# The weights of a block of keys in an mLSTM begun two units ahead of the products that read them

## The chip, the cores and the metric

The kernel runs on one core of a Trainium2 chip. It computes a whole encoder block for one sequence of 512 positions and a model width of 2048. The metric is the time of one execution on the device in microseconds (us), the median of several runs.

## The reference, cut to what matters

The block takes the root mean square norm of the input, projects it with one wide matrix, gives the columns to two branches (a Hyena branch of long convolutions and an mLSTM branch of 4 heads), merges the branches and ends with a gated feed-forward network. All is fp32. The change stands in the mLSTM branch, which runs forward and backward over the sequence:

```python
def mlstm_direction(q, k, v, i_pre, f_pre):
...
    dlog = b[..., :, None] - b[..., None, :] + ig[..., None, :]
    dlog = jnp.where(lower, dlog, -jnp.inf)
...
    s = jnp.einsum('bhcjd,bhcsd->bhcjs', qc, kc) * jnp.exp(dlog - m_j[..., None])
    inter_w = jnp.exp(inter - m_j)
    num = (jnp.einsum('bhcjs,bhcsv->bhcjv', s, vc)
           + inter_w[..., None] * jnp.einsum('bhcjk,bhcvk->bhcjv', qc, C_prev))
    den = jnp.sum(s, axis=-1) + inter_w * jnp.einsum('bhcjk,bhck->bhcj', qc, n_prev)
    h = num / jnp.maximum(jnp.abs(den), jnp.exp(-m_j))[..., None]
```

The reference works in chunks of 128 with a carried state. The kernel does a head in the closed form that this unrolls to: each query sees every key up to it (or from it on, backward), with the weight q·k/16 times the exponential of a difference of gate sums. With 512 positions there are 4 blocks of 128 keys, and the denominator is had from a column of ones that stands beside v.

## The kernel before, in words

**Products.** An fp32 product is done as three matmuls of split operands (`mm3`, lines 85 to 88): every operand is held as a rounded high part and the rest as a low part. ScalarE casts the high part, VectorE subtracts to get the low one, TensorE multiplies high by high, high by low, low by high. All these matmuls carry line 83 in the profile. The tiles tell them apart: `mm` are the sums of the projection in PSUM, `sd` those of the side work.

**Two streams.** The main stream is the projection, `w_in_cols`: group by group of 256 weight columns, one unit of the stream being 12 matmuls of 128x512 (2 blocks of 128 columns, 2 of 128 rows, 3 matmuls each). Its weights come by DMA and are split (lines 182 and 183) two units ahead of their use, into 4 buffers each for `wh` and `wl`. The side stream is the Hyena and mLSTM work on what the projection has delivered. `drive` (line 291) runs one projection unit, then lets the side stream go on until what it yields adds up to 2.6 per unit: the numbers that `mlstm` yields are the price of the piece just written, and so the order in which the two streams' instructions are written down. A scheduler then sets each engine's order: by when, in its own plan of the execution, the operands of an instruction are there, and, where several are, by the order of writing.

**A head.** `mlstm(h)` (line 893) does a head: it splits q and k (line 948 splits v), makes S, 4 blocks of q·k products, then works through 8 units, 4 blocks of keys forward and 4 backward. Unit n has two parts:
- `weights` (line 953) makes the weights of the block of keys: the exponential (line 957, ScalarE, over 512 to 128 columns), a select that puts zeros over the triangle of the block's own 128 columns (line 960, GpSimd), the product with S (line 962, VectorE), the cast to the high part `pH` (line 965, ScalarE) and the subtraction for the low part `pL` (line 966, VectorE). This is a chain of five over three engines; its tiles are `g`, from a pool of 24.
- The products (line 987): for the block of queries of the unit, over the blocks of keys so far, `mm3` of 128x258 into one `sd` tile. That is 1, 2, 3, 4 block products forward and the same backward, 20 in a head, 60 matmuls. After them the sum is divided: line 990 (ScalarE, into `dn`), 991 and 992 (VectorE), then line 995 (ScalarE, forward) or 997 (VectorE, backward, added to the forward result). Line 1003 transposes the result of the head.

In the loop (line 972) unit n writes the chain of unit n + 1 first and then its own products. So the chain of a unit is written one unit ahead of its products, and the chain of unit 0 before the loop. Each unit yields 1.5, the part before the loop 1.

**Where the heads lie.** In the profile the four heads' units run at 389.8 to 416 us (head 0, between two convolutions), 662.7 to 699 (head 1), 723 to 751 (head 2) and 766 to 786 (head 3). During head 1 another side stream, `combos_x` (line 1070), works as well: it prepares operands for the merge of the branches with VectorE's lines 1065 to 1084. Its operations and the mLSTM's take turns.

Of the kernel before, what the change touches and what calls it, by code (L numbers as in the profile page):

```python
# [34 lines left out]
def hybrid_block_kernel(ctx, tc, x, norm1_w, w_in, conv_w, conv_b, filt_w1, filt_b1, filt_freq1,  # L35
# [43 lines left out]
    def sd_ps():  # L79
        return new(psd, "sd")  # L80
# [4 lines left out]
    def mm3(o, aH, aL, bH, bL, start, stop):  # L85
        mm(o, aH, bH, start, False)
        mm(o, aH, bL, False, False)
        mm(o, aL, bH, False, stop)
# [273 lines left out]
    def gt(dt=F32, shape=(P, L)):  # L362
        t = vt(dt)[:, 0:2, 0:258].rearrange("p b c -> p (b c)")[:, 0:L]
        return t if len(shape) == 2 else t.rearrange("p (b c) -> p b c", b=shape[1])

    def vt(dt=F32R):
        n_tile[0] += 1
        return pr.tile([P, 2, 258], dt, tag="g", name=f"g_{n_tile[0]}", bufs=NG)
# [9 lines left out]
    def gsplit(src, shape=(P, L)):  # L378
        h = gt(F32R, shape)
        l = gt(F32R, shape)  # L380
        nc.scalar.copy(h, src)
        nc.vector.tensor_tensor(l, src, h.bitcast(F32), ALU.subtract)
        return h, l
# [498 lines left out]
    def fetch_qk(h):  # L882
        raw = []
        for src in (d_q, d_k):
            for j in range(2):
                t = gt()
                nc.gpsimd.dma_start(t, src[2 * h + j])
                raw.append(t)
        return raw
# [3 lines left out]
    def mlstm(h, following=None):  # L893
        yield from need("gates")
        if h in fetched_qk:
            raw = fetched_qk.pop(h)
        else:
            yield from need(("qk", h))
            raw = fetch_qk(h)
            yield "pause"  # L900
        qs, ks = [], []
        for dst in (qs, ks):
            for j in range(2):
                dst.append(gsplit(raw.pop(0)))
                yield .7

        def load_row(d):
            t = gt()
            nc.gpsimd.dma_start(t, d_rows[4 * d + h:4 * d + h + 1].to_broadcast([P, L]))
            return t  # L910

        def load_v():
            raw = []
            for b in range(2):
                t = gt()
                nc.gpsimd.dma_start(t.rearrange("p (b c) -> p b c", b=2),
                                    d_v[h][2 * b:2 * b + 2].rearrange("b p c -> p b c"))
                raw.append(t)
            return raw

        early = ("v", h) in done
        if early:
            raw = load_v()
            row = load_row(0)
        yield "pause"
        S = []
        for sb in range(4):
            ps = sd_ps()
            ss = slice(sb * P, (sb + 1) * P)
            for j in range(2):  # L930
                mm3(ps, ks[j][0][:, ss], ks[j][1][:, ss], qs[j][0], qs[j][1], j == 0, j == 1)
            t = gt()
            nc.scalar.activation(t, ps, AF.Copy, scale=1.0 / 16)
            S.append(t)
            yield .3
        if not early:
            yield from need(("v", h))
            raw = load_v()
            row = load_row(0)
            yield "pause"  # L940
        V = []
        for t in raw:
            vh, vl = vt(), vt()
            nc.gpsimd.memset(vh[:, :, 256:258].bitcast(F32), 1.0)
            nc.gpsimd.memset(vl[:, :, 256:258].bitcast(F32), 0.0)
            src = t.rearrange("p (b c) -> p b c", b=2)
            nc.scalar.copy(vh[:, :, 0:256], src)
            nc.vector.tensor_tensor(vl[:, :, 0:256], src, vh[:, :, 0:256].bitcast(F32), ALU.subtract)
            for k in range(2):
                V.append((vh[:, k, :], vl[:, k, :]))  # L950
            yield .7

        def weights(d, sb, row):

            js = slice(sb * P, L) if d == 0 else slice(0, (sb + 1) * P)
            e = gt()
            nc.scalar.activation(e[:, js], row[:, js], AF.Exp, bias=a_col[:, d, sb, h:h + 1], scale=-1.0)
            own = e[:, sb * P:(sb + 1) * P]
            sign = 1 if d == 0 else -1
            nc.gpsimd.affine_select(own, own, pattern=[[sign, P]], compare_op=ALU.is_ge, fill=0.0,  # L960
                                    base=0, channel_multiplier=-sign)
            nc.vector.tensor_tensor(e[:, js], e[:, js], S[sb][:, js], ALU.mult)  # L962
            pH = gt(F32R)
            pL = gt(F32R)
            nc.scalar.copy(pH[:, js], e[:, js])
            nc.vector.tensor_tensor(pL[:, js], e[:, js], pH[:, js].bitcast(F32), ALU.subtract)
            return pH, pL


        units = [(0, sb) for sb in (0, 1, 2, 3)] + [(1, sb) for sb in (3, 2, 1, 0)]  # L970
        acc_t = [gt(), gt()]
        nxt = weights(*units[0], row)
        row_b = load_row(1)
        yield 1
        W = {}
        for n, (d, jb) in enumerate(units):
            if n == 4:
                W = {}
            if n == 5 and ("qk", following) in done:
                fetched_qk[following] = fetch_qk(following)  # L980
            W[jb] = nxt
            if n < 7:
                nxt = weights(*units[n + 1], row if n < 3 else row_b)
            num = sd_ps()
            js = slice(jb * P, (jb + 1) * P)
            for i, (sb, (pH, pL)) in enumerate(W.items()):
                mm3(num[:, 0:258], pH[:, js], pL[:, js], *V[sb], i == 0, i == len(W) - 1)
            n_tile[0] += 1
            dn = pr.tile([P, 1], F32, tag="dn", name=f"dn_{n_tile[0]}", bufs=3)
            nc.scalar.activation(dn, num[:, 256:257], AF.Abs)  # L990
            nc.vector.tensor_scalar(dn, dn, em_col[:, d, jb, h:h + 1], None, ALU.max)
            nc.vector.reciprocal(dn, dn)
            to = acc_t[jb // 2][:, (jb % 2) * 256:(jb % 2) * 256 + 256]
            if d == 0:
                nc.scalar.activation(to, num[:, 0:256], AF.Copy, scale=dn)
            else:
                nc.vector.scalar_tensor_tensor(to, num[:, 0:256], dn, to, ALU.mult, ALU.add)
            yield 1.5
        for vb in range(2):
            ps = sd_ps()  # L1000
            for tb in range(4):
                c0 = (tb % 2) * 256 + vb * P
                nc.tensor.transpose(ps[:, tb * P:(tb + 1) * P], acc_t[tb // 2][:, c0:c0 + P], ident)  # L1003
            t = gt()
            nc.scalar.copy(t, ps)
            nc.gpsimd.dma_start(d_yb[2 * h + vb], t)
        yield .3
# [4 lines left out]
    def need(key):  # L1012
        while key not in done:
            yield "wait"

    def stream_a():
        yield from gate_rows()
        yield from need("filter")
        for kind, n in (("hy", 0), ("hy", 1), ("hd", 0), ("hy", 2), ("hy", 3)):
            yield from hyena(n) if kind == "hy" else mlstm(n)  # L1020
        ph_cm.__exit__(None, None, None)
        ts_pool.append(ts_cm.__enter__())
        done.add("ts")
        for h in (1, 2, 3):
            yield from mlstm(h, h + 1)
# [555 lines left out]
    W = {}  # L1581
# [87 lines left out]
```

## Time and profile before

| what | us |
|---|---|
| time before, median of 3 runs | 2853.32 |
| lowest and highest run | 2851.6, 2856.09 |
| the profiled execution, its own time | 2850.45 |
| its span on the core | 2848.7 |

The granted clock of TensorE over the profiled span is 0.998 of full speed. The profile shows one execution: which engine was busy when, with the source line and the tiles, and what ended the idle time before an instruction. PE is TensorE, PEld its loading of weights, DVE VectorE, ACT ScalarE, POOL GpSimd, SP SyncE. A group of instructions reads as line, engine, operation, tile written, tile read, shape. A matmul's duration is from its start to a modelled end, so matmuls in a row overlap: the pace is had from the starts of a long row, not from the mean duration.

### The profile page before, as it was taken

The page shows a single profiled execution, that of the slowest core. Times are in us where ns is not written, and L with a number is a line of the kernel's source. Part 1 is how long each engine was busy: PE and PEld are TensorE (multiplying, and loading weights), DVE is VectorE, ACT ScalarE, POOL GpSimd, SP SyncE. Part 2 cuts the span into 40 slices and gives each one's busy share as a digit, 9 for nine tenths or more (in the row PEclk, how much of TensorE's full clock was granted, in tenths as well). Part 3 has the DMA queues.
Part 4 walks back from the last instruction along what each step waited for, and adds up shares of the span by engine and source line. Part 5 has one row for each costly group of instructions (what it writes and reads, how often), then busy time and mean ns, then how long its engine had stood idle before and what let it go on. Part 6 is the DMA issues. An engine that isn't in the chain of part 4 may idle for free.

```text
span 2848.7 us, 47425 instructions
## 1 busy us (share of the span) xinstructions
PE 2824.8 (99%) x18028; PEld 2554.1 (90%) x18028; DVE 2110.6 (74%) x3844; ACT 1271.9 (45%) x2259; POOL 186.2 (7%) x431
## 2 busy tenths in 40 slices
PE   9999999999999999999999999999999999999998
PEld 7888878888889999888899999999999998888886
DVE  7898869888579898454459999999998995233336
ACT  5434453446645555232445444444444454232224
POOL 0101121012100001000110000000000000000000
PEclk9999999999999999999999999999999999999999
DMA  5334443344344434643443343333433436343433
GB/s 182 114 120 127 129 133 116 118 135 151 116 140 148 136 124 153 243 141 98 146 150 121 119 129 122 118 116 122 130 119 119 127 108 211 97 133 118 125 112 126
DMA packets 281490, 376.97 MB, mean 132 GB/s; under 512 B 18620, under 2 KB 214660, under 8 KB 281261
## 3 DMA queue, kind: packets, MB, share of 16 engines
q1 hardware_dynamic: 257243, 298.36, 34.1%
q0 software_dynamic: 22752, 73.44, 7.4%
q8 instruction: 141, 2.31, 0.3%
q10 hardware_dynamic: 1266, 2.13, 0.2%
q14 instruction: 88, 0.72, 0.1%
HBM read 326.67 MB, written 47.20 MB: 131 GB/s over the span
## 4 chain that ended last, share of the span: by engine, by line
PE 71%; DVE 1%; DMA 0%; ACT 0%; issue 0%; ACTq 0%
PE mm L83 50%; PE sd L83 21%; DMA wr<-in_w_down_dram 0%; PE sd L1395 0%; DVE h L93 0%; ACT h L92 0%; DVE wl L183 0%; DVE T L1423 0%; ACT bt L1397 0%; PE sd L1003 0%; DVE x L1596 0%; ACT sq L1599 0%; ACT x L1608 0%; DVE g L962 0%; DVE x L1600 0%
## 5 line engine op out<-in xcount | busy, mean ns | idle before, releaser
L183 DVE TENSOR_TENSOR wl<-wr,wh 128x512 fp32r<-128x512 f32 x512 | 350.0, 688 | 453.6 <-ACT wh L182 445.2
L182 ACT CAST wh<-wr 128x512 fp32r<-128x512 f32 x512 | 316.4, 622 | 733.0 <-PE mm L83 672.9
L83 PE MATMUL mm<-a,wh 128*128 128x512 f32 (+1 forms) x1816 | 564.5, 391 | 0.0
L83 PEld LDWEIGHTS mm<-a,wh 128*128 128x128 f32 x1816 | 337.9, 189 | 66.7 <-issue 0.8
L83 PE MATMUL mm<-a,wl 128*128 128x512 f32 x908 | 354.4, 390 | 1.8 <-DVE wl L183 1.0
L83 PE MATMUL mm<-wh,h 128*128 128x512 f32 x1152 | 355.2, 389 | 0.0
L83 PE MATMUL mm<-T,wh 128*128 128x256 f32 x1976 | 350.8, 279 | 1.5 <-ACT T L1422 1.2
L83 PE MATMUL sd<-T,wh 128*128 128x256 f32 x1968 | 347.8, 279 | 0.0
L1110 ACT CAST wh<-a 128x512 fp32r<-128x512 f32 x371 | 230.4, 622 | 262.2 <-PE mm L83 118.6
L83 PEld LDWEIGHTS mm<-T,wh 128*128 128x128 f32 x1976 | 301.4, 188 | 2.3 <-ACT T L1422 1.5
L83 PEld LDWEIGHTS sd<-T,wh 128*128 128x128 f32 x1968 | 299.8, 188 | 0.0
L83 PE MATMUL mm<-wh,a 128*128 128x512 f32 (+1 forms) x1024 | 287.1, 364 | 0.0
L1111 DVE TENSOR_TENSOR wl<-a,wh 128x512 fp32r<-128x512 f32 x371 | 253.6, 687 | 41.3 <-ACT wh L1110 35.6
L83 PE MATMUL mm<-T,wl 128*128 128x256 f32 x988 | 276.0, 279 | 0.0
L83 PE MATMUL sd<-T,wl 128*128 128x256 f32 x984 | 274.7, 279 | 0.0
L83 PEld LDWEIGHTS mm<-wh,h 128*128 128x128 f32 x1152 | 216.3, 188 | 44.8
L83 PE MATMUL mm<-wl,h 128*128 128x512 f32 x576 | 224.1, 389 | 0.0
L83 PEld LDWEIGHTS mm<-wh,a 128*128 128x128 f32 x1024 | 184.3, 189 | 29.6
L83 PEld LDWEIGHTS mm<-a,wl 128*128 128x128 f32 x908 | 171.4, 189 | 36.9 <-DVE wl L183 1.4
L83 PE MATMUL mm<-wl,a 128*128 128x512 f32 (+1 forms) x512 | 185.9, 363 | 0.0
L83 PEld LDWEIGHTS mm<-T,wl 128*128 128x128 f32 x988 | 185.7, 188 | 0.0
L83 PEld LDWEIGHTS sd<-T,wl 128*128 128x128 f32 x984 | 184.9, 188 | 0.0
(398 smaller groups left out, 5215.9 us busy)
## 6 DMA issues: line engine op xcount, KB each, us to landing
wr<-in_w_in_dram SPq DMA_DIRECT2D x140, 512.0 KB, 3.6
wr<-in_w_down_dram SPq DMA_DIRECT2D x88, 512.0 KB, 3.6
wr<-in_w_gate_up_dram SPq DMA_DIRECT2D x76, 512.0 KB, 4.0
a<-in_w_gate_up_dram SPq DMA_DIRECT2D x75, 512.0 KB, 4.0
r<-in_w_in_dram SPq DMA_DIRECT2D x36, 512.0 KB, 4.3
wr<-in_w_out_dram SPq DMA_DIRECT2D x32, 512.0 KB, 3.6
r<-in_w_gate_up_dram SPq DMA_DIRECT2D x25, 512.0 KB, 4.0
d_h<-xo POOLq DMA_DIRECT2D x44, 256.0 KB, 2.3
```

What stands on the lines that cost most here:

```text
L83: nc.tensor.matmul(o, a, b, start=start, stop=stop)
L182: nc.scalar.copy(h, src)
L183: nc.vector.tensor_tensor(l, src, h.bitcast(F32), ALU.subtract)
L1110: nc.scalar.copy(h, a)
L1111: nc.vector.tensor_tensor(l, a, h.bitcast(F32), ALU.subtract)
```

## The change

The chain of weights is now written two units ahead of the products that read it. Before the loop a second chain, that of unit 1, is written, with one more `yield 1` between the two; in the loop unit n writes the chain of unit n + 2. `nxt`, which held the weights of one unit, is a list that holds up to two.

```diff
         acc_t = [gt(), gt()]
-        nxt = weights(*units[0], row)
+        nxt = [weights(*units[0], row)]
         row_b = load_row(1)
+        yield 1
+        nxt.append(weights(*units[1], row))
         yield 1
         W = {}
         for n, (d, jb) in enumerate(units):
@@ -978,9 +980,9 @@
...
-            W[jb] = nxt
-            if n < 7:
-                nxt = weights(*units[n + 1], row if n < 3 else row_b)
+            W[jb] = nxt.pop(0)
+            if n < 6:
+                nxt.append(weights(*units[n + 2], row if n < 2 else row_b))
```

The lines behind the loop's head are two further down in the changed kernel: line 990 is 992 there, 995 is 997, 1083 is 1085.

The order of the instructions on TensorE, VectorE, GpSimd and ScalarE differs in the four heads only. TensorE, VectorE and GpSimd have the same instructions as before, ScalarE two table loads more. Three places show what moves. Numbers behind a tile's name differ between the kernels, as tiles are counted in the order of writing.

The first is TensorE's order at the start of head 1. `mm` are the projection's sums, `a` its input, `wh` and `wl` its weights; `sd` is the head's first sum, g_6992 and g_6993 are the high and low part of the first unit's weights, g_7058 and g_7059 those of v. Before:

```order
L83 MATMUL mm_6785<-a_448,wh_6972 128x512 x2
L83 MATMUL mm_6785<-a_448,wl_6973 128x512
L83 MATMUL sd_7076<-g_6992,g_7058 128x258
L83 MATMUL sd_7076<-g_6993,g_7058 128x258
L83 MATMUL mm_7093<-a_217,wh_7005 128x512 x2
L83 MATMUL mm_7093<-a_217,wl_7006 128x512
L83 MATMUL sd_7076<-g_6992,g_7059 128x258
```

After:

```order
L83 MATMUL mm_7085<-a_286,wh_7088 128x512 x2
L83 MATMUL mm_7085<-a_286,wl_7089 128x512
L83 MATMUL sd_7165<-g_6992,g_7058 128x258
L83 MATMUL sd_7165<-g_6993,g_7058 128x258
L83 MATMUL sd_7165<-g_6992,g_7059 128x258
L83 MATMUL mm_7084<-a_315,wh_7111 128x512 x2
```

The three matmuls of the first unit stand 33 projection matmuls further on than before, and in one run.

The second is ScalarE's order in the same head. Line 405 and line 414 finish a projection group of the next head (414 is a silu), g_7166 or g_7157 is the exponential of the third unit of head 1. Before:

```order
L405 ACTIVATE st_7136<-pp_7089,cols_87 128x512
L957 ACTIVATE g_7166<-g_6846,a_col_547 128x256
L414 ACT_TABLE_LOAD
L414 ACTIVATE st_7116<-st_7116 128x512
L414 ACTIVATE st_7139<-st_7139 128x512
L182 CAST wh_7186<-wr_7148 128x512
```

After:

```order
L405 ACTIVATE st_7127<-pp_7080,cols_87 128x512
L414 ACT_TABLE_LOAD
L414 ACTIVATE st_7107<-st_7107 128x512
L957 ACT_TABLE_LOAD
L957 ACTIVATE g_7157<-g_6846,a_col_547 128x256
L414 ACT_TABLE_LOAD
L414 ACTIVATE st_7130<-st_7130 128x512
L965 CAST g_7161<-g_7157 128x256
```

The exponential stood ahead of the two silus and now stands between them, so that a table is loaded for it and another one behind it.

The third is TensorE's order in the backward half of head 2. g_7754 and g_7755 (after: g_7723 and g_7724) are the high and low part of the weights of one unit, g_7638 and g_7639 a block of v. Before:

```order
L83 MATMUL mm_7801<-a_350,wh_7924 128x512 x2
L83 MATMUL sd_7784<-g_7638,g_7754 128x258
L83 MATMUL sd_7784<-g_7639,g_7754 128x258
L83 MATMUL sd_7837<-g_7638,g_7754 128x258
L83 MATMUL sd_7837<-g_7639,g_7754 128x258
L83 MATMUL sd_7857<-g_7638,g_7754 128x258
L83 MATMUL sd_7857<-g_7639,g_7754 128x258
L83 MATMUL sd_7784<-g_7638,g_7755 128x258
L83 MATMUL sd_7837<-g_7638,g_7755 128x258
L83 MATMUL sd_7857<-g_7638,g_7755 128x258
L83 MATMUL sd_7888<-g_7638,g_7754 128x258
```

After:

```order
L83 MATMUL mm_7792<-a_347,wh_7908 128x512 x2
L83 MATMUL sd_7820<-g_7638,g_7723 128x258
L83 MATMUL sd_7820<-g_7639,g_7723 128x258
L83 MATMUL sd_7845<-g_7638,g_7723 128x258
L83 MATMUL sd_7845<-g_7639,g_7723 128x258
L83 MATMUL mm_7792<-a_347,wl_7909 128x512
L83 MATMUL sd_7820<-g_7638,g_7724 128x258
L83 MATMUL sd_7845<-g_7638,g_7724 128x258
L83 MATMUL sd_7873<-g_7638,g_7723 128x258
L83 MATMUL sd_7873<-g_7639,g_7723 128x258
L83 MATMUL sd_7873<-g_7638,g_7724 128x258
L83 MATMUL mm_7792<-a_350,wh_7908 128x512 x2
```

The matmuls that read this unit's weights stood in one unbroken run of twelve, of which the first ten are shown; now a projection matmul stands between those that read the high part and those that read the low part, and another behind.

## The prediction

> **What bounds the kernel now.** I read the page first: who is busy, and on whom the chain that ended last stands.
>
> ```profile
> span 2848.7 us, 47425 instructions
> PE 2824.8 (99%) x18028; PEld 2554.1 (90%) x18028; DVE 2110.6 (74%) x3844; ACT 1271.9 (45%) x2259; POOL 186.2 (7%) x431
> PE 71%; DVE 1%; DMA 0%; ACT 0%; issue 0%; ACTq 0%
> ```
>
> TensorE is busy for 99% of the span. A change on the other engines can only move the time by making TensorE wait more or less often. So the question is how long TensorE waits in the stage of the change, and the waits of TensorE's weight loads by reason tell where to look.
>
> ```profile
> PEld sd L83 <- ACT g L965: 8.2, 21, 0.8
> PEld sd L83 <- DVE g L966: 1.8, 6, 0.6
> ```
>
> The columns are the total in us, how often, and the longest. The block products (line 83, into `sd`, reading `g`) wait 21 times for the cast at line 965 and 6 times for the subtraction at line 966, the two halves of a unit's weights. Such a wait of the weight loader partly lies beside a matmul that still runs, so these 10.0 us are not yet lost time. To get that I take TensorE's pace and hold the four heads' stretches of block products against it. The pace is in the chain that ended last, the stretches in a table of windows (length, TensorE busy with its matmuls counted, granted clock, DMA share, GB/s).
>
> ```profile
> 788.74 30.91 PE mm L83 x147
> 840.49 19.60 PE sd L83 x168
> 1134.50 217.62 PE mm L83 x960
> ```
>
> ```profile
> 395.80:414.70 18.90, 18.29 (x99) 1.00 0.32 98
> 667.60:699.30 31.70, 31.33 (x165) 1.00 0.52 156
> 725.60:751.60 26.00, 25.84 (x136) 1.00 0.42 132
> 768.60:786.10 17.50, 17.40 (x100) 1.00 0.26 75
> ```
>
> With nothing to wait for, a 128x512 product takes 217.62/960 = 0.2267 us and a 128x256 one 19.60/168 = 0.1167; for 258 columns I scale the latter by 258/256, 0.1176 (an estimate). A head has 20 block products of 3 matmuls, 60 x 0.1176 = 7.06 us; the rest of each count are projection matmuls of 128x512. The rest of each window is lost:
> head 0, 18.90 - 7.06 - 39 x 0.2267 = 3.00; head 1, 31.70 - 7.06 - 105 x 0.2267 = 0.84; head 2, 26.00 - 7.06 - 76 x 0.2267 = 1.71; head 3, 17.50 - 7.06 - 40 x 0.2267 = 1.37. **Together 6.9 us, 0.24% of the span: the most that any edit of these waits can gain.** The measurement of this kernel can tell about 0.2%, 5.7 us, from no change.
>
> Also, there is no tail to shorten: in the chain the projection goes on without a gap from 788.74 to 819.65, when the side work is over (the last head's transposes, line 1003, stand before 788).
>
> **The change part by part.** *The order of writing.* Per head, 8 chains are written as before (exp, select, product with S, cast, subtraction), the first two before the loop; unit n + 2's chain is now written ahead of unit n's products. The same matmuls, casts and subtractions run; in the order of each engine only the four heads differ. Cost by itself: nothing.
>
> *Outside head 1.* What is written is not what runs: a scheduler puts each instruction where its operands are ready in its own plan. In the rows of TensorE's order (shown above with the change) the block products stand directly behind the cast that they read, in both versions: the chain is begun sooner, but its products are taken sooner too, and the loop's products then stand in more and shorter runs between projection matmuls. I counted the unbroken runs of block products in TensorE's order: heads 0, 1, 2, 3 had 12, 8, 11 and 10, and have 12, 7, 16 and 12. What TensorE loses arises where such a run begins: it has to wait for its first operand.
>
> ```profile
> 395.71 0.39 PE L83 MATMUL mm<-a,wh 128*128 128x512 f32 x1
> 396.29 1.23 PE L83 MATMUL sd<-g,g 128*128 128x258 f32 x8 [0.19 <-ACT g L965]
> 397.91 0.74 PE L83 MATMUL sd<-g,g 128*128 128x258 f32 x4 [0.40 <-DVE g L966]
> 398.49 0.40 PE L83 MATMUL mm<-a,wl 128*128 128x512 f32 x1
> ```
>
> These are head 0's first two runs: the product at 396.29 starts 0.58 us behind the one at 395.71 where 0.23 is the pace, and the one at 397.91 waits again. Heads 0, 2 and 3 lose 3.00 + 1.71 + 1.37 = 6.1 us in 33 runs, 0.18 us each. After, they have 40 runs; seven more at 0.18 is **+1.3 us**. The ends: at head 0's price, 3.00/12 = 0.25 for each of the 40 runs, they would lose 10.0, +3.9; and if all the waits in these heads were gone, -6.1. I take +1.3 because the runs in the order still begin right behind their casts, as at 396.29.
>
> *Head 1.* Here the projection stretch is longer, and TensorE's loss is one late chain:
>
> ```profile
> 667.25 0.39 PE L83 MATMUL mm<-a,wl 128*128 128x512 f32 x1
> 668.01 0.50 PE L83 MATMUL sd<-g,g 128*128 128x258 f32 x2 [0.37 <-ACT g L965]
> 668.35 0.63 PE L83 MATMUL mm<-a,wh 128*128 128x512 f32 x2
> ```
>
> The product at 668.01 starts 0.76 behind 667.25 where 0.23 is the pace. What made it late stands on GpSimd and VectorE:
>
> ```profile
> 663.54 3.04 POOL L960 TENSOR_SCALAR_AFFINE_SELECT g<-g 128x128 f32<-128x128 f32 x1 [4.83 <-ACT g L957]
> 664.14 0.68 DVE L948 TENSOR_TENSOR g<-g,g 128x512 fp32r<-128x512 f32 x1
> 664.74 1.08 DVE L1084 TENSOR_TENSOR T<-g,T 128x256 fp32r<-128x256 f32 x3
> 666.61 0.69 DVE L962 TENSOR_TENSOR g<-g,g 128x512 f32<-128x512 f32 x1 [0.19 <-POOL g L960]
> ```
>
> ```profile
> L960 POOL TENSOR_SCALAR_AFFINE_SELECT g<-g x32: 286/292/3044, 390.6 to 783.8; 128x128 f32<-128x128 f32 x32
> ```
>
> One select of 32 took 3.04 us where 0.29 is the median (shortest, median, longest), while VectorE ran one instruction on another. In the new order these first products of head 1 stand 33 projection matmuls later, 33 x 0.2267 = 7.5 us, more than the 0.84 that they were late: the wait goes, **-0.8 us**. The ends are -0.84 and 0. The later products of head 1 wait for nothing that I could find in either order: they stand rows behind their casts.
>
> *Two more table loads.* In head 1 the exponential of unit 2 now stands between two silus (line 414), so ScalarE loads a table for it and another back.
>
> ```profile
> 673.48 0.50 ACT L957 ACTIVATE g<-g,a_col 128x256 f32<-128x256 f32 x1
> 673.99 1.28 ACT L414 ACT_TABLE_LOAD   x1
> 675.28 1.37 ACT L414 ACTIVATE st<-st 128x512 f32<-128x512 f32 x2
> 676.56 0.60 ACT L182 CAST wh<-wr 128x512 fp32r<-128x512 f32 x1
> ```
>
> The load starts 0.01 us behind the exponential and the silu 0.01 behind the load: 1.3 us per switch, two are 2.6 us of ScalarE. Queued behind them are the cast of line 965 and the projection's next cast (line 182). The projection's casts are two units of 12 matmuls ahead, 24 x 0.2267 = 5.4 us, more than 2.6; and ScalarE has room:
>
> ```profile
> 660.00:703.00 43.00, 42.63 (x215) 35.79 (x214) 40.45 (x96) 31.54 (x65) 10.15 (x21) 1.00 0.45 135
> ```
>
> (After the length: TensorE, its loader, VectorE, ScalarE, GpSimd.) ScalarE is idle for 11.5 of 43.0 us. I take 0; without that cover it is +2.6.
> The Trainium skill, on the page "ScalarE: Activation LUTs" in the section "What ACT_TABLE_LOAD costs", adds a drain of about 1.38 us to each load, so an estimate by that page is 5.3 us for the two switches, just the cover's size. The rows above show no drain on either side of this load.
>
> **Sum.** +1.3 - 0.8 + 0 = +0.5 us on the profiled 2850.45: 2850.9. The median of the runs, 2853.32, lies 2.9 above the profiled run, so I give **2853.8**: no change that can be measured. Its own range, from the ends: -6.1 - 0.8 to +3.9 + 2.6, with most of the weight in the middle, and the runs of before themselves lie 4.5 us apart.
>
> **The rivals.**
> *A, the chain is hidden (faster).* If the hardware reaches the products later than the plan believes, a chain begun one unit earlier has a unit more time, and all the waits go: -6.9, 2846.4. For it: on hardware each chain that runs ahead of its plan shortens the next wait. Against it: the products moved with the chains, and a unit's own time is short (head 0 does 8 units in 18.9 us, 2.4 us each), and any smaller part of the 6.9 stays below 5.7. It has to remove over 80% of the waits to be seen. Chance 0.07.
>
> *B, the selects stretch (slower).* Two chains are now under way at once, so a select (GpSimd) of one falls more often on VectorE's product or subtraction of the other. At the stretch at 663.54 a select takes 3.04 - 0.29 = 2.75 us longer. In heads 0, 2 and 3 the products stand at most three projection matmuls (0.68 us) behind their cast, so each stretch costs TensorE 2.1 to 2.7 us. From three of the 24 selects there on it is measured: 3 x 2.5 = +7.5, 2861.3. For it: the one stretch in the trace, and the overlap. Against it: 31 of 32 took their 0.29 us although VectorE was busy beside them too, and it took some 3 us of unbroken VectorE work; VectorE has gaps in those heads, as in head 0's:
>
> ```profile
> 385.00:420.00 35.00, 34.39 (x173) 26.97 (x172) 21.97 (x51) 20.66 (x45) 7.54 (x23) 1.00 0.29 83
> ```
>
> VectorE is busy for 22.0 of 35.0 us there. Chance 0.09.
> The Trainium skill says on the page "SBUF — State Buffer", section "Who interferes with whom", that a VectorE instruction with two inputs in SBUF contends with a GpSimd instruction that reads SBUF, and that the loser blocks fully. The line of VectorE work over the select at 663.54 agrees with it; the 31 short selects show that it is rare here.
>
> *C, the table loads are not covered:* +2.6, 2856.4, still within 0.2%; with one stretched select it would be measured. *D, the change doesn't do what it says:* the scheduler begins the chains no earlier in its plan, and only rows change places; ±0, 2853.3. Head 0's rows on ScalarE speak for it: the third exponential moves ahead of one evacuation (line 995) only. C and D lie in the forecast's interval, as variants of it.
>
> **How the numbers follow.** Forecast with C and D 0.84 (within 0.2%), A 0.07, B 0.09. The range of 8 in 10 lies inside the forecast's ends, cut where little weight is left: down, half of the waits gone with the head 1 gain (-3.5 - 0.8, about 2849.0), up, head 0's price for all runs (+3.9, about 2857.2, with a little of C and of B above it): 2849.0 to 2858.0.
>
> **What would show it.** Right: in the profile after, the four windows of block products, held against the same pace, lose some 7 us again, head 1 nearly nothing and head 2 more than its 1.71; one more table load each at lines 957 and 414, in head 1, and no wait of TensorE for line 182 or 183 there. Wrong: the waits for lines 965 and 966 together well below 5 us (A), or several selects of line 960 above 1 us with as many waits of 2 us behind them (B). Were the time to move by over 5.7 us with the four windows as before, the cause would lie outside these heads, and the step that says the rest of the order is the same would have failed.

## The result and the profile after

On the first occasion the changed kernel took 2860.45 us (median of 22 runs, 2851.55 to 2863.25), the kernel before 2854.70 us beside it (22 runs, 2847.86 to 2861.80). The ratio is 1.0018, 95% interval 1.0010 to 1.0026: slower by some 5 us. The forecast was 2853.8 us and no change, in a range from 2849.0 to 2858.0. On two later occasions the same pair gave 1.0001 (0.9993 to 1.0010) and 1.0015 (1.0004 to 1.0027). That the size depends on the occasion is part of the answer below. One run of the kernel before on a later occasion (e9) took 3423.53 us at a granted clock of 0.766, where all others have 0.979 to 0.999, and is left out of every figure.

The profiled execution after has a span of 2858.3 us, 9.6 us more than before, with the same matmuls. I set the start of one and the same matmul beside itself in the two traces: at 808.6 us before it comes 1.5 us later after, at 1490.7 us 1.7 us later, at 2377.9 us 9.6 us later, at the end 9.6. (At 100 us, where nothing has changed, this execution was 0.6 us ahead.) So there are two places: the heads, and a long stage far behind them that the change does not touch.

**The heads.** The windows from the last projection matmul ahead of a head's first block product to the first one behind its last (length, TensorE busy with its matmuls, clock, DMA share, GB/s), of before and of after:

```profile
395.70:414.87 19.17, 18.56 (x100) 1.00 0.33 101
667.24:697.50 30.26, 29.89 (x158) 1.00 0.49 148
725.53:752.03 26.50, 26.34 (x138) 1.00 0.42 130
768.53:785.85 17.32, 17.22 (x98) 1.00 0.26 76
```

```profile
395.09:413.26 18.17, 17.57 (x97) 1.00 0.34 102
674.76:701.46 26.70, 26.70 (x146) 1.00 0.54 168
724.08:750.78 26.70, 26.53 (x140) 1.00 0.41 129
767.22:786.78 19.56, 17.41 (x94) 0.91 0.23 67
```

One matmul of each count only runs over into the window. Of the rest, 60 are block products at 0.1176 us and the others projection matmuls at 0.2267: for head 3, 17.32 - 7.06 - 37 x 0.2267 = 1.9 us lost before and 19.56 - 7.06 - 33 x 0.2267 = 5.0 after. The loss of heads 0 to 3 goes from 3.3, 1.2, 2.0 and 1.9 us to 3.0, 0.4, 1.7 and 5.0. (The prediction's windows were cut a little differently, so its levels lie up to 0.5 lower; here both sides are cut alike.) Heads 0 and 2 gain 0.3 each, head 1 gains 0.8, head 3 loses 3.1: **+1.7 us**. The waits for the two halves of the weights show it as one longer wait:

```profile
PEld sd L83 <- ACT g L965: 8.4, 18, 2.6
PEld sd L83 <- DVE g L966: 1.7, 6, 0.6
```

Before, the longest of these was 0.8 us. The long one is the first product of head 3; TensorE in the profile after:

```profile
767.00 0.61 PE L83 MATMUL mm<-a,wh 128*128 128x512 f32 x2
769.76 2.95 PE L83 MATMUL sd<-g,g 128*128 128x258 f32 x12 [2.15 <-ACT g L965]
772.51 0.63 PE L83 MATMUL mm<-a,wl 128*128 128x512 f32 x1
```

The twelve products behind the wait take 2.75 us to the next start, 0.23 us each, where twelve took 1.66 before (768.95 to 770.61). The clock says why: a table of windows gives 0.50 for the 3.3 us from 769.7.

```profile
769.70:773.00 3.30, 3.24 (x14) 3.14 (x15) 2.05 (x5) 1.63 (x5) 0.37 (x1) 0.50 0.47 120
```

What came late is the row of the forward gates. GpSimd before and after, between heads 2 and 3 (before first):

```profile
755.08 1.10 POOL L1006 DMA_DIRECT2D d_yb<-g  x2 [4.96 <-ACT g L1005]
756.17 1.45 POOL L916 DMA_DIRECT2D g<-d_v  x2
757.62 0.57 POOL L909 DMA_DIRECT2D g<-d_rows  x1
761.00 1.09 POOL L462 DMA_DIRECT2D d_o<-st  x2 [2.81 <-ACT st L461]
```

```profile
753.83 1.10 POOL L1008 DMA_DIRECT2D d_yb<-g  x2 [6.61 <-ACT g L1007]
757.82 0.54 POOL L462 DMA_DIRECT2D d_o<-st  x1 [2.89 <-DVE g L382]
758.35 1.45 POOL L916 DMA_DIRECT2D g<-d_v  x2
759.80 0.57 POOL L909 DMA_DIRECT2D g<-d_rows  x1
760.36 0.56 POOL L462 DMA_DIRECT2D d_o<-st  x1
```

Both stores of line 462 stood behind the loads of head 3. Now one stands ahead of them, and GpSimd waits for its data (2.89 us idle) with the loads queued behind it. (The row names line 382; the store's data come from the silu of line 461, which ends 0.30 us ahead of the store here as it does before.) The row is fetched 2.2 us later (759.80 for 757.62), although TensorE comes to head 3 sooner than before. On ScalarE the exponential's table load then waits for that row:

```profile
763.10 1.30 ACT L947 CAST g<-g 128x512 fp32r<-128x512 f32 x2 [0.31 <-DMA g<-d_v]
765.95 1.28 ACT L957 ACT_TABLE_LOAD   x1 [1.55 <-DMA g<-d_rows]
767.25 0.72 ACT L957 ACTIVATE g<-g,a_col 128x512 f32<-128x512 f32 x1
```

Before, that load stood right behind the casts, at 765.13, without a wait. So 1.55 of the 2.15 us are the row's. The rest comes from TensorE being there sooner: its last projection matmul ahead of the product starts at 767.23 us, before at 768.54.

**The long stage.** From about 1525 us to 2359, in the changed kernel to 2368, runs the gate and up projection of the feed-forward network: some 7200 products of 128x256 from the wait at its start on, without a stop. The chain that ended last, before and after:

```profile
1535.78 19.60 PE mm L83 x168
1555.38 19.60 PE sd L83 x168
```

```profile
1537.60 19.79 PE mm L83 x168
1557.38 19.79 PE sd L83 x168
```

19.60/168 is 116.7 ns, 19.79/168 is 117.8: 1.1 ns on each of 7200 products is the other **7.9 us**. The order of all engines is the same there, TensorE waits for nothing in either, and the clock is 1.00 in both. In the starts of single products the first pace goes 120, 113, 116, 118, ... without repeating exactly, the second one repeats 116, 118, 119 ns. (In e5 and e12 below the stage at 116.7 ns repeats 116, 117, 117, so the pattern alone doesn't tell the paces apart.)

### The profile page after: what moved, and what is told of

It reads as the page before. It is cut to its first block, busy times and chain, and to the rows that moved or that the text cites. A ratio compares the mean times of both kernels' runs of the same rounds, so it can differ in the third digit from the quotient of the medians.

```text
span 2858.3 us, 47429 instructions
## 1 busy us (share of the span) xinstructions
PE 2832.2 (99%) x18028; PEld 2562.5 (90%) x18028; DVE 2115.0 (74%) x3844; ACT 1273.7 (45%) x2261; POOL 187.6 (7%) x431
## 4 chain that ended last, share of the span: by engine, by line
PE 95%; issue 2%; DVE 1%; DMA 1%; ACT 1%; POOL 0%; SPq 0%; POOLq 0%; DVEq 0%; ACTq 0%
PE mm L83 68%; PE sd L83 26%; DMA wr<-in_w_down_dram 0%; PE sd L326 0%; PE sd L764 0%; PE sd L1397 0%; DVE wl L183 0%; DMA g<-d_hy 0%; DMA xt<-in_x_dram 0%; DVE st L410 0%; DVE h L93 0%; DVE st L407 0%; PE sd L875 0%; ACT wh L182 0%; DVE g L564 0%
```

## The experiments

Theory A: the change costs what the late row of head 3 costs, less its gain in the other heads, and the rest of the difference is the pace of the stages of 128x256 products, which an execution draws when a wait ends. Its rivals: the extra `yield 1` is the cause; the code itself sets the pace (B); the change, or its lateness, makes the slow pace likelier (A2). These letters are those of the expectations below, not those of the prediction's rivals.

**e1, the kernel before, unchanged.**

> The kernel before, unchanged. Theory A (two paces): between about 1525 and 2330 us TensorE runs the 128x256 products either at 116.7 ns or at 117.8 ns each, fixed by how one short wait at the start of that stage ends, so executions of one and the same kernel fall into two groups some 8 us apart, near 2851 and near 2860; the profile shows either pace. The rival B (the code sets the pace): the kernel before always runs this stage at 116.7, as in its first profile, and only the changed kernel at 117.8. By both, the four heads' windows lose some 7 us and the third-longest wait is not in head 3.

Measured: 2851.09 us (11 runs, 2849.34 to 2860.50), ratio 1.0004 (0.9995 to 1.0013). The profile had 116.7 ns in the stage. On that occasion 7 of 35 runs of the kernel before were above 2857 us, 28 below 2854.2, none between: two groups, and one program. B does not explain them. The groups are not always parted so cleanly: of e1's own eleven runs one is at 2860.50 and one between, at 2855.06, and four of the 22 on the first occasion lie at 2856.1 to 2856.5.

**e2, only the extra yield.**

```diff
         nxt = weights(*units[0], row)
         row_b = load_row(1)
         yield 1
+        yield 1
```

> The kernel before with one more yield 1 ahead of the loop, the chains still one unit ahead. On GpSimd's queue the loads of head 3 (v, then the row) stand ahead of both stores of line 462, as in the kernel before. Theory A: no wait over 1 us in head 3, and the same times as before, in two groups. If the moved yield itself were the cause: head 3 waits 2 us and the time is as after the change.

Measured: 2850.13 us, ratio 1.0000 (0.9988 to 1.0013), 3 of 12 runs above 2857 us. No long wait in head 3; the first product there starts 0.39 us behind the matmul before it:

```profile
768.33 0.39 PE L83 MATMUL mm<-a,wl 128*128 128x512 f32 x1
768.72 1.47 PE L83 MATMUL sd<-g,g 128*128 128x258 f32 x9
```

**e3, two units ahead without the extra yield.**

```diff
         nxt = [weights(*units[0], row)]
         row_b = load_row(1)
-        yield 1
         nxt.append(weights(*units[1], row))
         yield 1
```

> The change without its extra yield. On GpSimd's queue one store of line 462 stands ahead of the loads of head 3, as in the changed kernel. Theory A: the wait of about 2.3 us at the first product of head 3 comes again, with the granted clock at half speed for some 3 us behind it, together 3 to 4 us; the later stage at either pace. If the extra yield made the wait, it is gone here and the time is that of before.

Measured: 2854.37 us, ratio 1.0010 (0.9997 to 1.0022). The wait is there:

```profile
767.81 0.61 PE L83 MATMUL mm<-a,wh 128*128 128x512 f32 x2
770.41 0.89 PE L83 MATMUL sd<-g,g 128*128 128x258 f32 x3 [1.98 <-ACT g L965]
```

So the lookahead brings it, not the yield. The profiled execution had the slow pace of the long stage (19.79 us for 168) and was 11.1 us longer than the first of before; 3 of 12 runs lay above 2857 us.

**e4, the change with the row fetched at the start of the head.**

```diff
+        row = load_row(0)
         qs, ks = [], []
...
-            row = load_row(0)
...
-            row = load_row(0)
```

> The change, with the row of the forward gates fetched at the start of each head, ahead of the store that it stood behind; nothing else moved. Theory A: the wait of 2.3 us in head 3 and the half clock behind it are gone, so 3 to 4 us less than the changed kernel at the same pace of the later stage: near 2848 with 116.7 ns there and near 2856 with 117.8. Were the select or the cast the cause, the wait would stay.

Measured: 2852.09 us, ratio 1.0009 (0.9998 to 1.0020), 4 of 12 runs above 2857 us; the profiled execution fell on the slow pace. The 3 to 4 us that were expected can't be told in the times: the medians of e3 and e4 lie 2.3 us apart, and the runs of each scatter over some 13 us. The store still stands ahead of the loads of v and waits for its data, but head 3's first product waits 0.8 us only (1.26 us behind the start of two matmuls that take 0.45), and the clock holds:

```profile
767.68 0.61 PE L83 MATMUL mm<-a,wh 128*128 128x512 f32 x2
768.94 1.83 PE L83 MATMUL sd<-g,g 128*128 128x258 f32 x12 [0.64 <-ACT g L964]
```

In the source only the row was moved, so the row was the late operand; 0.64 us of the 2.15 are left with the row early. At the end of the heads this kernel lies 0.2 us before the kernel before, the changed one 1.5 behind.

**e5, the changed kernel again.**

> The changed kernel, unchanged, on another occasion. Theory A (the pace of the gate and up products between 1525 and 2330 us is a matter of the single execution): its runs again fall into two groups, near 2852.5 with 116.7 ns per product and near 2860.5 with 117.8, as in the kernel before, and the profile may show either; head 3 waits 2.3 us in both. Theory A2 (the change makes the slow pace more likely): three of four runs or more in the upper group again. Rival B (the code sets the pace): all runs near 2860.

Measured: 2852.32 us, ratio 1.0001 (0.9993 to 1.0010), none of 12 runs above 2857, so the expected upper group did not appear. The profile of the very same program has a span of 2849.0 us, 9.3 less than its first one, and here is its long stage:

```profile
1535.72 19.60 PE mm L83 x168
1555.32 19.60 PE sd L83 x168
```

That rejects B. The first product of head 3 waits here too, 1.51 us by the row below, but the twelve products then take 1.54 us to the next start (the clock stayed at 1.00):

```profile
770.01 1.70 PE L83 MATMUL sd<-g,g 128*128 128x258 f32 x12 [1.51 <-ACT g L965]
771.55 0.39 PE L83 MATMUL mm<-a,wl 128*128 128x512 f32 x1
```

**e6, the changed kernel with three short transposes in the long stage**, and **e7, the kernel before with one.** They write a half of a PSUM bank that nobody reads.

```diff
+            if mark:
+                nc.tensor.transpose(bk[3][:, 256:384], ident, ident)
             product(p4, a22, "4")
...
-        U = gate_up.cols(FH + f * P, sd_ps)
+        U = gate_up.cols(FH + f * P, sd_ps, mark=f in (0, 14, 28))
```

> The changed kernel with one more 128x128 transpose on TensorE, into an unused half of a PSUM bank, in the gate and up stage at its 1st, 8th and 15th of 22 pairs of column groups. It changes no value that is read. Theory A: such a short instruction between the products lets TensorE fall into a pace anew, so the pace can differ between the three stretches that it parts; if the pace behind a transpose is always 116.7 (as behind the transposes at 1512 us in all six profiles so far), no run is in the upper group and the median is near 2852.5, 8 us below the changed kernel's slow runs, at a cost of 3 x 0.11 us. If the pace is set from outside, the transposes change nothing.

> The kernel before with one such transpose, in the first pair of column groups of the stage. Theory A, with the pace behind a transpose always 116.7: all runs in the lower group, 2848 to 2853, none near 2859; this would beat both kernels on the mean. If the lock is struck by chance at the transpose too: a part of the runs in the upper group as before.

Measured: e6 2856.30 us, ratio 1.0015 (1.0006 to 1.0024), 5 of 12 runs above 2857 us; e7 2851.80, 1.0001 (0.9989 to 1.0012). In e6's one execution the pace changes at a transpose (line 1178) and changes back at the next:

```profile
1774.00 19.60 PE mm L83 x168
1793.60 16.80 PE sd L83 x144
1810.40 0.11 PE sd L1178
...
1833.12 19.79 PE sd L83 x168
...
2110.05 19.60 PE sd L83 x168
```

So a short interruption is enough to draw the pace anew, and the outcome is not always the quick one: that half of the expectation failed, and e7 still had one run at 2860.65. Both profiles also show the slow pace in another stage, the merge (825 to 1114 us), where some 2450 products make it 2.7 us dearer, as do those of e13 and e15. It is of the same kind, with its own draw.

**e8, the kernel before, 2.1 us later from the merge on** (19 such transposes in its first column groups).

> The kernel before with 19 transposes of 128x128 in the first column groups of the merge, about 2.1 us of TensorE's time: all behind 822 us comes as much later as with the change, the heads are as before. Theory A: two groups, 2.1 us above those of the kernel before, and the share of the upper group as in it. Theory A2, with the lateness as the cause: most runs in the upper group, near 2861.

Measured: 2854.85 us, ratio 1.0011 (0.9998 to 1.0025), 3 of 12 runs above 2857 us with the 2.1 us included. Lateness alone does not bring the slow pace.

**e9 and e10, the two kernels again, beside each other.**

> The kernel before, unchanged, beside the changed kernel on one chip. Theory A (two paces, in the merge stage, 825 to 1114 us, and in the gate and up stage, 1525 to 2330 us, drawn when a wait ends): most runs at 2848 to 2854, some near 2859; the share of these, 20% on the last two occasions, need not be that of the first occasion. Heads' windows lose some 7 us.

> The changed kernel, unchanged. Theory A: the same two groups with about the same share of slow paces as the kernel before beside it, and 0.5 to 2 us longer by the late row of head 3 (a wait of 1.6 to 2.4 us, with or without the half clock behind it): a median 0.5 to 3 us above the kernel before. Theory A2 (the change makes the slow pace likelier): half of the runs or more above 2857, as on the first occasion.

Measured: e9 2852.93 us (11 runs), ratio 0.9999 (0.9985 to 1.0012), e10 2855.31 us, 1.0015 (1.0004 to 1.0027). Above 2857 us lay 5 of e9's 11 runs, 10 of the 35 of the kernel before beside them and 5 of 12 of the changed one: nothing here for A2. e10's profile has the quick pace in both stages and still a span of 2853.3 us, 4.5 more than e9's; 3.0 of them are there at 808.6 us, and its first product of head 3 waited longest of all.

```profile
768.25 0.61 PE L83 MATMUL mm<-a,wh 128*128 128x512 f32 x2
771.63 0.63 PE L83 MATMUL sd<-g,g 128*128 128x258 f32 x3 [2.77 <-ACT g L965]
```

**e11, two units ahead in head 1 alone.**

```diff
+        two = h == 1
+        if two:
+            nxt.append(weights(*units[1], row))
+            yield 1
...
-            if n < 6:
-                nxt.append(weights(*units[n + 2], row if n < 2 else row_b))
+            if n < 7 - two:
+                nxt.append(weights(*units[n + 1 + two], row if n < 3 - two else row_b))
```

> The chains two units ahead in head 1 alone, with its extra yield; heads 0, 2 and 3 as before, and on GpSimd's queue the loads of head 3 ahead of both stores of line 462 as before. Theory A: head 1's wait of 0.5 us behind the long select is gone (0.8 us won), head 3 waits under 0.3 us as before, so 0.8 us less than the kernel before at equal paces, no difference that can be measured. If lookahead in head 1 alone delays what follows it, head 2 or 3 waits longer.

Measured: 2855.52 us, ratio 1.0002 (0.9991 to 1.0014), 5 of 12 runs above 2857 us. In its profile head 1 loses 0.3 us for 1.2, the heads end 0.6 us sooner than before, and the long stage fell on 117.8 ns, with the chains of heads 0, 2 and 3 one unit ahead. The slow pace needs none of what the change does there.

**e12, the kernel before without the wait at the start of the long stage.** In the profile of before a product waits there for the low part of its operand (line 1111), whose cast stands on ScalarE behind two silus:

```profile
1520.70 1.15 ACT L1506 ACTIVATE xo<-xo 128x512 f32<-128x512 f32 x2
1521.76 0.60 ACT L1110 CAST h<-a 128x512 fp32r<-128x512 f32 x1
...
1523.14 0.39 PE L83 MATMUL sd<-T,a 128*128 128x256 f32 x1
1523.37 0.40 PE L83 MATMUL sd<-T,h 128*128 128x256 f32 x2
```

(These are rows of two engines; 0.23 us lie between the starts of the last two for 0.117 elsewhere.) The edit writes the first pair's silus behind the products:

```diff
         for t in G:
             nc.vector.tensor_tensor(t, t, norm2["bc"], ALU.mult)
-            nc.scalar.activation(t, t, AF.Silu)
+            if f:
+                nc.scalar.activation(t, t, AF.Silu)
         U = gate_up.cols(FH + f * P, sd_ps)
+        for t in G if f == 0 else ():
+            nc.scalar.activation(t, t, AF.Silu)
```

> The kernel before with the first pair's two silus in the gate and up stage written behind the products that follow them, so that the cast of the operand for which TensorE waits at 1523 us comes some 0.5 us sooner. Theory A, with the pace of that stage drawn when this wait ends: the wait (0.14 instead of 0.117 us, then 0.22) is gone, the stage goes on at the 116.7 ns that it has had behind the transposes just ahead in all ten profiles, and no run is 8 us longer than the others; only the merge's pace (2.7 us) still scatters. If the pace is drawn elsewhere, some runs are near 2859 as before.

Measured: 2850.89 us, all 11 runs between 2849.59 and 2853.78, ratio 0.9991 (0.9982 to 0.9999). One of the two silus moved, the wait is gone, and the products run at 116.7 ns from the last transposes ahead of the stage to its end:

```profile
1523.71 0.28 PE L83 MATMUL sd<-T,a 128*128 128x256 f32 x1
1523.82 0.40 PE L83 MATMUL sd<-T,h 128*128 128x256 f32 x2
```

**e13, e14, e15: that edit in the kernel before, in the changed kernel, and in the changed kernel with the early row.** With the groups 8 us apart gone, the change's own price can be measured.

> The kernel before without the wait at the start of the gate and up stage, as in the last experiment, as the base for the next two. Theory A: again no run near 2859, all within some 5 us, the median near 2851.

> The changed kernel, also without that wait. Theory A (the change's own price is the late row of head 3 less the gain in heads 0 to 2): no run 8 us above the others, and the median 1 to 3 us above the base beside it. Theory A2 (the change itself brings the slow pace of the stage): a part of the runs near 2860 all the same. The rival that the change costs nothing of its own: within 0.7 us of the base.

> The changed kernel without that wait and with the row of each head fetched at the head's start. Theory A: the price of head 3 goes, 2 to 3 us below the changed kernel without the wait, and 0.5 us below the base, which is within what can be measured.

| kernel, 12 runs each on one chip | median us | lowest to highest | mean, standard deviation |
|---|---|---|---|
| e13, before | 2850.91 | 2847.61 to 2854.17 | 2851.04, 1.97 |
| e14, changed | 2852.43 | 2848.92 to 2855.78 | 2852.61, 1.80 |
| e15, changed, early row | 2850.46 | 2848.80 to 2853.21 | 2850.96, 1.55 |

None of the 36 runs is above 2857 us; of the kernel before, on the same occasion, 11 of 29 were. The means say that the change costs 1.6 us of its own (plus or minus 1.5, twice the standard error of the difference) and that the early row takes 1.6 off again (plus or minus 1.4). Against the kernel before, e13 has 0.9990 (0.9980 to 1.0001), e14 0.9995 (0.9984 to 1.0005) and e15 0.9989 (0.9978 to 1.0000). e12, e13 and e15 are the quickest kernels of this study, by about 0.1% on average, since they never pay the 8 us (the interval stays below 1 for e12 alone); among themselves they don't differ.

## Why the prediction was wrong, point by point

- **The bound of the gain held, the step "cost by itself: nothing" failed.** It said that the same matmuls, casts and subtractions run and that only the four heads differ in the order of each engine, and went on to TensorE, ScalarE and GpSimd's selects. It did not follow the loads of the next head on GpSimd's queue. There one store, which waits for its data, came to stand ahead of them. The prediction named a row fetched late in no rival. Its rival B, the stretched selects, had the right size of a single event (2 to 3 us of TensorE) and the wrong instruction: in the profile after no select outside head 1 took over 0.5 us. Its ground that 31 of 32 took their 0.29 us was off as well: in the profile before five of these took 0.39 to 0.58 us, each begun while VectorE ran an instruction on two tiles.
- **The term "+1.3 us outside head 1" had the wrong sign in heads 0 and 2** (-0.3 each) and missed head 3 (+3.1). The number of runs of products is no measure of the loss; each run's wait has its own cause.
- **Head 1 held:** its loss fell by 0.8 us as forecast. The long select came again (2.96 us at 662.66), and TensorE did not wait for it.
- **The table loads held:** two loads of 1.28 us stand ahead of the exponential at 674.95 and one behind it, and TensorE lost 0.4 us in all of head 1's window. The Trainium skill, on the page "ScalarE: Activation LUTs" in the section "What ACT_TABLE_LOAD costs", adds a drain to each switch; in these rows the instruction behind a load starts 0.01 to 0.02 us after its end, so no such drain showed here.

```profile
671.71 1.28 ACT L414 ACT_TABLE_LOAD   x1
...
673.66 1.28 ACT L957 ACT_TABLE_LOAD   x1
674.95 0.51 ACT L957 ACTIVATE g<-g,a_col 128x256 f32<-128x256 f32 x1
675.48 1.28 ACT L414 ACT_TABLE_LOAD   x1
676.77 0.63 ACT L414 ACTIVATE st<-st 128x512 f32<-128x512 f32 x1
```

- **The clock was left out.** A wait was priced by its length alone. In head 3 the clock then fell to 0.50, which cost about 1.1 us more on the first twelve products alone.
- **The step "can only move the time by making TensorE wait" failed, and the scatter was taken for noise of 4.5 us, from three runs.** The long stage took 7.9 us more although TensorE waited no longer there. The runs of the kernel before reach from 2847.7 to 2863.3 us over all occasions, in groups some 8 us apart, and the median depends on how many of them fall into the upper one. On the first occasion 19 of 22 runs of the changed kernel and 7 of 22 of the kernel before did (above 2857 us), on the two later ones 0 of 12 and 5 of 12 beside 6 of 35 and 15 of 46. Twelve more of 22 runs at 8 us are 4.4 us (an estimate); with the 1.6 us of the change's own that is 6.0, where 5.1 was measured and the 1.6 is uncertain by 1.5. So the larger part of the measured difference is a matter of that occasion: on the two later ones the changed kernel's medians, 2852.32 and 2855.31 us, lie inside the forecast's range. The sum of the prediction, +0.5 us, is wrong by about 1 us as to the program; its range was too narrow for the pace.

What stays open: why the changed kernel met the slow pace in 19 of 22 runs on the first occasion. Twelve more such runs than the kernel before had are too many to be put down to luck without a reason. Later runs of it did not repeat that, e11 shows the pace without the change in three of four heads, e8 that lateness doesn't bring it; what decides the draw was not found. Whether the chip has a part in it was not tested; the four later occasions ran on four different ones.

## What to carry to other kernels

When a stream of work is written in another order, look at what its neighbours on every queue are afterwards, those of the loads of the next piece above all: a store that waits for its data holds up every load behind it on the same queue (here for 2.89 us). Before a difference of 0.2% is explained, look for groups in the runs of the unchanged kernel, and set the same matmul of two traces beside itself to see in which stage the time arose. A stage of thousands of equal matmuls is a lever of its own: one wait of about 0.1 us at its start decided over 8 us.

## What the runs showed of the hardware

- The long rows of 128x256 fp32 products in the merge and in the gate and up stage have two steady paces at a granted clock of 1.00, 116.7 and 117.8 ns. In all seventeen profiles they kept one pace until the next interruption, over up to 7,200 products, and three transposes changed it twice in one execution. Behind the transposes at 1512 us, without the wait, it was 116.7 in all four profiles of e12 to e15.
- The clock fell to half for 3.4 us behind the wait at head 3's first product in five profiles, with 1.75 to 2.77 us of idle (the first profile after, e3, e6, e10, e14), and not in e5, with 1.51. At the merge's start, behind two waits with 1.08 and 0.77 us of idle one after the other, it fell in ten of the seventeen profiles, the first one of before among them, and not in the others, e1 among them, which then were 1.5 us quicker there. So what a wait of 1 to 2 us costs is a draw, too.

```profile
823.10:826.10 3.00, 3.00 (x16) 0.51 0.35 121
```

```profile
822.80:826.00 3.20, 3.20 (x29) 1.00 0.42 145
```

The first row is of before, the second of e1, the same program: 16 matmuls in 3.0 us and 29 in 3.2.
